# The output projection of an attention layer as seven half-size products instead of a plain product in eight quarters of the weights

## The chip, the cores and the metric

The kernel runs on one core of a Trainium2 chip. The metric is device time in microseconds (us) of one execution. TensorE does the matrix products and accumulates in PSUM; VectorE (DVE) and ScalarE (ACT) do elementwise work; GpSimd (POOL) and SyncE (SP) mostly issue DMA transfers here. Each engine works through a queue of its own in the order in which the program put the instructions there, and an instruction that waits holds everything behind it on that engine.

## The reference, cut to what matters

The model has two residual layers over 512 tokens and 1024 features. Layer 0 mixes tokens by pooling, layer 1 by attention; after each mixer comes a gated feed-forward. The change touches the last step of the attention mixer, the product of the merged heads (512 x 1024) and `w_out` (1024 x 1024):

```
merged = jnp.concatenate(
    [o_g * (N_ATTN_GROUPS * alpha[:, :, g]).astype(o_g.dtype)[:, :, None, None] for g, o_g in enumerate(outs)],
    axis=2,
).reshape(B, S, D_ATTN)
return jnp.einsum('bse,ed->bsd', merged, w_out)
...
        x = x + y
        h = rmsnorm(x, norm_ffn[i])
        x = x + swiglu(h, ffn_w_gate[i], ffn_w_up[i], ffn_w_down[i])
```

## The kernel before

All data are 32-bit floats. To keep their accuracy, each operand of a large product is split into a high part (a cast by ACT, `whi`, `bhi` or `h`) and the rest (a subtraction by DVE, `wlo`, `blo` or again `h`), and a product takes three matmuls: high by high, high by rest, rest by high. Weights pass through a queue of items of 128 x 1024 numbers (512 KB): SP loads an item into one of five buffers `wraw`, and `weights()` splits some items ahead of their use. A buffer is loaded again when its rest has been taken.

The feed-forwards already save products by a Strassen scheme (seven half-size products for eight). For it some items are sums of weight blocks, made by a DMA that adds into its destination, issued by POOL (`accum_op=ALU.add`; tiles `wraw` or `vraw`, line 138, and line 180 where one buffer is added to again after each split).

The end of the attention layer goes as follows. POOL writes the softmax weights of all heads to DRAM (`far`) and reads them back, spread over rows, into the tiles `LB0` to `LB2` and `even_rows` (line 1250). `merged(t)` for t = 0 to 7 takes the products of probabilities and values of two heads on TensorE (lines 1332 and 1334; eight products through four PSUM banks `mm`). DVE multiplies each by the weights (lines 1338 and 1342), and the result, 128 features x 512 tokens, is split into `m_hi` and `m_lo`, which are the memory of `h` (lines 387 and 388). Then `out_projection` runs: for the first 512 output columns it goes through four items of weights, each against four blocks of 128 tokens, and for the last 512 columns through four blocks of tokens, each against four items that stay split (`bhi`, `blo`). That makes 192 matmuls of 128x512 (lines 425 to 427). DVE adds each finished bank to the residual `x` (line 413), and the norm of the feed-forward follows block by block: squares (line 324), multiplication by the gain (line 333), inverse root mean square (lines 339 to 343), scaling (line 352), and transposes on TensorE (lines 366 and 358). The first feed-forward product (line 729) is next.

TensorE's order is the order in which the program is written. On the other engines a scheduler lays out the queue from its own costs and from priorities (`high_priority`).

## Time and profile before

| What | Value |
|---|---|
| median of 3 runs | 981.42 us (980.79 to 981.96) |
| the profiled execution: its time, its span | 980.24 us, 978.5 us |
| TensorE, DVE, ACT, POOL busy | 99%, 80%, 59%, 13% of the span |
| mean granted TensorE clock | 0.999 |
| DMA traffic | 163.00 MB, mean 167 GB/s |

The span is the time from the first to the last instruction of the core, and the 1.74 us between it and the execution's time lie around it. Times inside a run are counted from the span's start. A row of the timeline gives start, duration, engine, line, operation, output and inputs, a count (x2 where rows are merged), and in brackets how long the engine was idle before and what ended that. A row of the chain of waits gives start, length, engine, tile and line. The line numbers of the rows are those of the kernel before.

### The profile page before, as it was taken

Reading aid. Unit: us, or ns where it says so; the run is one execution under the profiler, and the core shown is the slowest. Engines: PE = TensorE matmul, PEld = TensorE weight load, DVE = VectorE, ACT = ScalarE, POOL = GpSimd, SP = SyncE. Lnnn points to the kernel's source line nnn. Section 1 sums busy time; section 2 is a strip of 40 time slices with the busy share of each in tenths; the row PEclk is TensorE's granted clock in tenths of the full one; section 3 lists DMA queues with packets and bytes.
Section 4 is the critical chain, followed back from the end, with each engine's and each line's share of the span. In section 5 each row is a group of like instructions: output and inputs, shape, how many; then the busy total and the mean of one; then the engine's idle time right before and its main releaser. Section 6 shows DMA issues by size and latency. Waiting matters only on the chain.

```text
span 978.5 us, 15597 instructions
## 1 busy us (share of the span) xinstructions
PE 970.9 (99%) x6028; PEld 862.6 (88%) x6028; DVE 783.9 (80%) x1083; ACT 575.3 (59%) x903; POOL 124.7 (13%) x124
## 2 busy tenths in 40 slices
PE   9999999999999999999999999999999999999997
PEld 8888899988988999889888899899998998899886
DVE  6475799888888888797897547579988898888876
ACT  6573566655665666574553554366664675567655
POOL 0002010010011111101212124101011101110110
PEclk9999999999999999999999999999999999999999
DMA  9448267479668877555221249627657947987652
GB/s 346 176 157 207 45 187 186 124 200 248 165 151 222 218 201 159 117 193 165 86 79 55 62 137 295 115 59 204 174 145 205 251 111 173 250 213 193 153 134 101
DMA packets 79466, 163.00 MB, mean 167 GB/s; under 512 B 6096, under 2 KB 6480, under 8 KB 79392
## 3 DMA queue, kind: packets, MB, share of 16 engines
q1 hardware_dynamic: 58544, 122.04, 37.6%
q0 software_dynamic: 20560, 39.69, 23.7%
q8 instruction: 47, 0.77, 0.3%
q14 instruction: 27, 0.22, 0.1%
q10 hardware_dynamic: 288, 0.27, 0.1%
HBM read 159.85 MB, written 2.13 MB: 166 GB/s over the span
## 4 chain that ended last, share of the span: by engine, by line
PE 99%; ACT 0%; DVE 0%; issue 0%; ACTq 0%
PE pair L703 32%; PE pair L847 21%; PE p L729 5%; PE mm L264 5%; PE mm L266 4%; PE mm L265 4%; PE pair L729 4%; PE r L729 2%; PE early L515 2%; PE mm L425 2%; PE mm L427 2%; PE mm L426 2%; PE mm L729 1%; PE mm L1297 1%; PE mm L1298 1%; PE mm L1299 1%
## 5 line engine op out<-in xcount | busy, mean ns | idle before, releaser
L175 DVE TENSOR_TENSOR wlo<-wraw,whi 128x1024 fp32r<-128x1024 f32 (+2 forms) x190 | 221.7, 1172 | 65.6 <-ACT whi L171 65.0
L171 ACT CAST whi<-wraw 128x1024 fp32r<-128x1024 f32 (+2 forms) x189 | 184.0, 979 | 138.4 <-PE pair L703 27.8
L171 ACT CAST whi<-vraw 128x1024 fp32r<-128x1024 f32 (+1 forms) x108 | 105.2, 980 | 117.6 <-DVE vraw L177 39.8
L175 DVE TENSOR_TENSOR wlo<-vraw,whi 128x1024 fp32r<-128x1024 f32 (+1 forms) x108 | 121.5, 1133 | 46.2 <-ACT whi L171 46.2
L703 PE MATMUL pair<-h,whi 128*128 128x512 f32 (+1 forms) x640 | 143.2, 349 | 0.0
L703 PEld LDWEIGHTS pair<-h,whi 128*128 128x128 f32 x640 | 109.1, 188 | 13.4
L703 PE MATMUL pair<-t,whi 128*128 128x512 f32 (+1 forms) x512 | 110.6, 337 | 0.0
L847 PE MATMUL pair<-whi,u_hi 128*128 128x512 f32 (+1 forms) x284 | 109.9, 387 | 0.0
L847 PE MATMUL pair<-wlo,u_hi 128*128 128x512 f32 (+1 forms) x284 | 109.9, 387 | 0.0
L847 PE MATMUL pair<-whi,u_lo 128*128 128x512 f32 (+1 forms) x284 | 109.7, 386 | 0.0
L703 PEld LDWEIGHTS pair<-t,whi 128*128 128x128 f32 x512 | 86.1, 190 | 8.4
L703 PE MATMUL pair<-h,wlo 128*128 128x256 f32 x512 | 89.2, 281 | 0.0
L703 PEld LDWEIGHTS pair<-h,wlo 128*128 128x128 f32 x512 | 76.1, 188 | 4.2
L138 POOL DMA_DIRECT2D wraw<-w x22 | 26.6, 1211 | 396.0 <-DMA wraw<-w 123.2
L177 DVE TENSOR_TENSOR vraw<-vraw,wraw 128x1024 f32<-128x1024 f32 (+1 forms) x66 | 75.2, 1139 | 0.7
L703 PE MATMUL pair<-t,wlo 128*128 128x256 f32 x384 | 71.9, 282 | 0.0
L264 PE MATMUL mm<-h,whi 128*128 128x512 f32 (+1 forms) x176 | 64.3, 365 | 0.0
L266 PE MATMUL mm<-h,wlo 128*128 128x512 f32 (+1 forms) x176 | 63.4, 360 | 0.0
L265 PE MATMUL mm<-h,whi 128*128 128x512 f32 (+1 forms) x176 | 63.4, 360 | 0.0
L847 PEld LDWEIGHTS pair<-whi,u_lo 128*128 128x128 f32 x284 | 53.3, 188 | 10.9
L847 PEld LDWEIGHTS pair<-whi,u_hi 128*128 128x128 f32 x284 | 53.4, 188 | 10.4
L847 PEld LDWEIGHTS pair<-wlo,u_hi 128*128 128x128 f32 x284 | 53.4, 188 | 10.2
(363 smaller groups left out, 2021.4 us busy)
## 6 DMA issues: line engine op xcount, KB each, us to landing
wraw<-w SPq DMA_DIRECT2D x116, 512.0 KB, 4.7
wraw<-w_down SPq DMA_DIRECT2D x32, 512.0 KB, 4.2
vraw<-w SPq DMA_DIRECT2D x22, 512.0 KB, 4.8
wraw<-w POOLq DMA_DIRECT2D x22, 512.0 KB, 6.9
vraw<-w POOLq DMA_DIRECT2D x22, 512.0 KB, 9.1
wraw<-wT SPq DMA_DIRECT2D x16, 512.0 KB, 4.4
vraw<-w_down POOLq DMA_DIRECT2D x12, 512.0 KB, 6.5
wraw<-w_down SPq DMA_DIRECT2D x24, 256.0 KB, 3.3
```

The source lines that it names most:

```text
L138: nc.gpsimd.dma_start(dst, more, accum_op=ALU.add)
L171: nc.scalar.copy(hi[:, :n], raw[:, :n])
L175: nc.vector.tensor_sub(lo[:, :n], raw[:, :n], hi[:, :n].bitcast(F32))
L177: nc.vector.tensor_add(raws[into][:, :n], raws[into][:, :n], raws[more][:, :n])
L264: nc.tensor.matmul(ps, lhsT=whi, rhs=xhi, start=first, stop=False, **kw)
L265: nc.tensor.matmul(ps, lhsT=whi, rhs=xlo, start=False, stop=False, **kw)
L266: nc.tensor.matmul(ps, lhsT=wlo, rhs=xhi, start=False, stop=last, **kw)
L425: nc.tensor.matmul(ps, lhsT=xhi, rhs=w[0][:, k, :], start=first, stop=False)
L426: nc.tensor.matmul(ps, lhsT=xhi, rhs=w[1][:, k, :], start=False, stop=False)
L703: mat = lambda o, w, m, **kw: nc.tensor.matmul(o, lhsT=w, rhs=m, skip_group_check=True, **kw)
L729: nc.tensor.matmul(ps[:, g, :], lhsT=w[:, g, c, :], rhs=right[:, z, c, :], start=i in (0, 1, 3) and g + c + k == 0, stop=c == 3 and k == 2 ...
L847: nc.tensor.matmul(acc(t), lhsT=u, rhs=w, start=first, stop=n == len(places) - 1, skip_group_check=True)
```

## The change

The projection becomes seven products of half the tokens (256), half the features (512) and half the columns (512). Write a1 and a2 for the first and second half of the tokens in the first 512 features, b1 and b2 in the last 512, and W(m,k) for the block of the weights at column half m and feature half k. The left operands are a2, a2-a1, a1-a2-b1, b1, b1-a1, b2 and a2-a1+b1-b2, formed by DVE (class `Left`). The right operands are W(0,0), W(1,0)+W(1,1), that plus W(0,0), that plus W(0,1), W(0,0)+W(1,0), W(0,1) and W(1,1). They run in the order `SEVEN` = 0, 1, 2, 5, 4, 3, 6, each as two items of weights (z = 0 in `whi`/`wlo`, z = 1 in `bhi`/`blo`). Products 1, 2 and 5 share two buffers `sraw`: after product 1's item is split, a DMA adds W(0,0) to the same buffer for product 2, and after that one's split W(0,1) for product 5. Products 0, 2, 4 and 6 accumulate in one pair of banks (`p`, in the rows `sc`), 1 and 5 in another (`r`, `mm`), 3 alone in a third (`q`, `tp`), and after each product DVE adds or subtracts both its banks to or from `x` (`flush`). The flag `SEVEN_OUT = (False, True)` selects this for the attention layer alone; layer 0 keeps its code path.

```
+SEVEN = (0, 1, 2, 5, 4, 3, 6)
+SEVEN_OUT = (False, True)
...
+            for z in range(2):
+                block = lambda m, k: by[:, order[2 * k + z] : order[2 * k + z] + 2, COLS[m]]
+                src = {0: [(0, 0)], 1: [(1, 0), (1, 1)], 3: [(0, 1)], 4: [(0, 0), (1, 0)], 6: [(1, 1)]}.get(i)
+                item = dict(kind="w" if src else "sum", shape=(2, S), rows=True, ahead=8, **({"pool": "b"} if z else {}))
...
+                if i in (1, 2):
+                    item["loads"] = (js[1][z] if i == 2 else len(queue), block(0, i - 1))
...
+        def second(self):
+            t = self.raw[0]
+            with tc.high_priority(URGENT):
+                nc.vector.tensor_sub(self.spare, t[:, :, SECOND], t[:, :, FIRST])
+                self.split(1, self.spare)
...
+                if i is None:
+                    self.next_sum(FIRST)
+                    self.split(2, self.spare)
+                    self.split(5, more[:, :, FIRST])
+                    nc.vector.tensor_sub(t[:, :, FIRST], more[:, :, FIRST], t[:, :, FIRST])
+                elif i == 0:
+                    self.split(6, t[:, :, FIRST])
+                elif i == 1:
+                    self.split(3, more[:, :, SECOND])
+                    self.next_sum(SECOND)
...
+        product(1)
+        product(2)
+        product(5)
+        for b in range(2):
+            norm.square(b, 0)
+            norm.gained(b, 0)
+        left.reserve()
+        product(4)
+        for b in range(2):
+            norm.square(b, 1)
+            norm.gained(b, 1)
+            norm.prepare(b)
+        product(3)
+        for t in range(2):
+            norm.square(2 + t, 0, q[t])
+        rests = turned_rows(norm, shift, list(enumerate(tps())))
+        ws = operands(6)
+        rests()
...
-            o = scaled_by[t % 4]
+            o = raw[t // 4][:, t % 4, :] if seven else scaled_by[t % 4]
...
+                    if t in (1, 3):
+                        left.first(t - 1)
+                    elif t == 4:
+                        left.second()
+                    elif t == 7:
+                        left.behind(None)
...
-        third = out_projection(j_wo, range(NC), m_hi, m_lo, norm, SHIFT, four, turned_banks)
+            third = seven_projection(j_wo, left, norm, SHIFT, p, r, q, lambda: (more, r), lambda: None, False)
```

Up to the end of the attention's value products the queues of all engines are as before, but for DMA issues on SP and POOL. What changes on DVE and POOL is shown at three places. In the rows, `LB` and `even_rows` are the spread weights of the heads, `pT` after the change holds the merged heads and their sums, `h` the split left operands, `sc`, `mm` and `tp` PSUM banks of the projection, `wraw` a loaded item of the projection or of the feed-forward.

DVE before, from the first merged pair of heads on:

```order
L1338 TENSOR_TENSOR o_5837<-mm_5839,LB0_5262 128x512
L388 TENSOR_TENSOR h_74<-o_5837,h_74 128x512
L1338 TENSOR_TENSOR o_5838<-mm_5859,LB1_5263 128x512
L388 TENSOR_TENSOR h_74<-o_5838,h_74 128x512
L1338 TENSOR_TENSOR odd_rows_81<-mm_5879,LB2_5264 128x512
L1342 TENSOR_TENSOR odd_rows_81<-mm_5899,even_rows_5826 128x4x128
L388 TENSOR_TENSOR h_74<-odd_rows_81,h_74 128x512
L1342 TENSOR_TENSOR o_5837<-mm_5911,even_rows_5826 128x4x128
```

DVE after, from the same place to the last merged pair:

```order
L1538 TENSOR_TENSOR pT_4231<-mm_5828,LB0_5262 128x512
L1538 TENSOR_TENSOR pT_4231<-mm_5846,LB1_5263 128x512
L183 TENSOR_TENSOR wlo_5968<-sraw_5957,whi_5967 128x1024
L423 TENSOR_TENSOR h_74<-pT_4231,h_74 128x512
L1538 TENSOR_TENSOR pT_4231<-mm_5866,LB2_5264 128x512
L1542 TENSOR_TENSOR pT_4231<-mm_5884,even_rows_5817 128x4x128
L1542 TENSOR_TENSOR pT_4231<-mm_5896,even_rows_5817 128x4x128
L522 TENSOR_TENSOR pT_4231<-pT_4231 128x1024
L423 TENSOR_TENSOR h_74<-pT_4231,h_74 128x512
L1542 TENSOR_TENSOR pT_4231<-mm_5909,LB0_5262 128x4x128
L423 TENSOR_TENSOR h_74<-pT_4231,h_74 128x1024
L1542 TENSOR_TENSOR pT_4231<-mm_5919,LB1_5263 128x4x128
```

The rest of product 1's first item (`wlo<-sraw`) now stands between the second and the third pair; the third pair's bank is read behind it. After the last row come the last pair (`LB2`), the rest of product 1's second item (`blo<-sraw`), the third sum of the left operands (line 526), its rest, the fifth sum (line 538) and the rest of b1.

DVE after, where the first products end (behind the rows just named):

```order
L578 TENSOR_TENSOR x_72<-sc_5949,x_72 128x512
L578 TENSOR_TENSOR x_72<-sc_5950,x_72 128x512
L423 TENSOR_TENSOR h_74<-pT_4231,h_74 128x1024
L580 TENSOR_TENSOR x_72<-x_72,mm_5953 128x512
L580 TENSOR_TENSOR x_72<-x_72,mm_5954 128x512
L423 TENSOR_TENSOR h_74<-pT_4231,h_74 128x1024
L526 SCALAR_TENSOR_TENSOR pT_4231<-pT_4231 128x1024
L183 TENSOR_TENSOR wlo_5978<-sraw_5957,whi_5977 128x1024
L183 TENSOR_TENSOR blo_5983<-sraw_5960,bhi_5982 128x1024
L183 TENSOR_TENSOR wlo_5991<-sraw_5957,whi_5990 128x1024
L183 TENSOR_TENSOR wlo_6032<-wraw_5987,whi_6031 128x1024
L578 TENSOR_TENSOR x_72<-sc_5949,x_72 128x512
```

DVE before, at the corresponding place:

```order
L388 TENSOR_TENSOR h_74<-o_5838,h_74 128x512
L388 TENSOR_TENSOR h_74<-odd_rows_81,h_74 128x512 x2
L175 TENSOR_TENSOR wlo_6112<-wraw_6099,whi_6111 128x1024
L175 TENSOR_TENSOR wlo_6116<-wraw_6101,whi_6115 128x1024
L175 TENSOR_TENSOR wlo_6120<-wraw_6107,whi_6119 128x1024
L175 TENSOR_TENSOR wlo_6124<-wraw_6109,whi_6123 128x1024
L413 TENSOR_TENSOR x_72<-sc_5963,x_72 128x512
```

The rests of product 2's two items (`wlo_5978`, `blo_5983`) and of product 5's first (`wlo_5991`) stand behind the flushes of products 0 and 1; before, only rests of feed-forward weights stood here. After the last row shown come the other flush of product 2 and the rest of product 5's second item.

POOL after, from the write of the heads' weights (the rows `sraw` with L144 add W(1,1), those with L188 add for products 2 and 5):

```order
L1432 DMA far_5266<-ropea_5722 64x128
L1438 DMA LB0_5262<-far_5266 64x512 x2
L1438 DMA LB1_5263<-far_5266 64x512 x2
L1438 DMA LB2_5264<-far_5266 64x512 x2
L1438 DMA even_rows_5817<-far_5266 64x512 x4
L144 DMA sraw_5957<-wT 128x2x512
L144 DMA sraw_5960<-wT 128x2x512
L1438 DMA LB0_5262<-far_5266 64x512 x2
L1438 DMA LB1_5263<-far_5266 64x512 x2
L188 DMA sraw_5957<-wT 128x2x512
L1438 DMA LB2_5264<-far_5266 64x512 x2
L188 DMA sraw_5960<-wT 128x2x512
```

POOL before, there:

```order
L1244 DMA far_5266<-ropea_5722 64x128
L1250 DMA LB0_5262<-far_5266 64x512 x2
L1250 DMA LB1_5263<-far_5266 64x512 x2
L1250 DMA LB2_5264<-far_5266 64x512 x2
L1250 DMA even_rows_5826<-far_5266 64x512 x4
L1250 DMA LB0_5262<-far_5266 64x512 x2
L1250 DMA LB1_5263<-far_5266 64x512 x2
L1250 DMA LB2_5264<-far_5266 64x512 x2
```

Now the two first adds into `sraw` stand behind the four loads of `even_rows`, and an add that waits for a rest on DVE stands ahead of the last two loads of heads' weights (`LB2`). Ahead of `far`, two adds for product 4's items (`wraw`) are new, and behind the rows shown two more adds into `sraw` follow, for product 5.

More of the change, by code (lines that the diff above doesn't have):

```diff
@@ L154, in weights @@
         for n in range(loaded["w"], min(len(queue), i + load_ahead)):
+            if queue[n].get("sums") and "s" not in pools:
+                break
             if queue[n]["kind"] == "w":
@@ L462, in out_projection, with __init__, split, first @@
         return tps
+    class Left:
+        def __init__(self, raw, spare, places):
+            self.raw, self.spare, self.places = raw, spare, places
+        def split(self, u, src, ks=(slice(0, 4),)):
+            hi, lo = self.places[u]
+            for k in ks:
+                split(hi[:, k, :], lo[:, k, :], src[:, k, :])
+        def first(self, k):
+            self.split(0, self.raw[0][:, :, SECOND], (slice(k, k + 2),))
+        def second(self):
[3 more added lines that the diff above has]
+                self.split(1, self.spare)
+        def next_sum(self, part):
+            nc.vector.scalar_tensor_tensor(
+                self.spare, self.spare, -1.0, self.raw[1][:, :, part], op0=ALU.mult, op1=ALU.subtract
+            )
+        def behind(self, i):
+            t, more = self.raw
+            with tc.high_priority(URGENT):
+                if i is None:
[8 more added lines that the diff above has]
+                    self.next_sum(SECOND)
+                elif i == 4:
+                    self.split(4, self.spare)
+        def reserve(self):
+            if 4 not in self.places:
+                self.places[4] = [
+                    wspl.tile([P, 1024], F32R, name=name).rearrange("p (k s) -> p k s", k=4) for name in ("whi", "wlo")
+                ]
@@ new lines, in seven_projection, with operands, products, flush @@
+    def seven_projection(js, left, norm, shift, p, r, q, tps, after_first, keep):
+        accs = {0: p, 1: r, 2: p, 3: q, 4: p, 5: r, 6: p}
+        def operands(i):
+            return [weights(j, split_ahead=6, held=z + (i in (4, 3, 6))) for z, j in enumerate(js[i])]
+        def products(i, ws, ts=range(2)):
+            hi, lo = left.places[(0, 1, 2, 3, 6, 5, 4)[i]]
+            places = [(z, t, c) for z in range(2) for t in ts for c in range(2)]
+            for z, t, c in places:
+                whi, wlo = (w[:, c, :] for w in ws[z])
+                uhi, ulo = (u[:, 2 * z + c, t * P : (t + 1) * P] for u in (hi, lo))
+                for k, (u, w) in enumerate(((uhi, whi), (uhi, wlo), (ulo, whi))):
+                    first, last = (i < 2 or i == 3 and not keep) and (z, c, k) == (0, 0, 0), (z, c, k) == (1, 1, 2)
+                    nc.tensor.matmul(accs[i][t], lhsT=u, rhs=w, start=first, stop=last, skip_group_check=True)
+        def flush(i, t):
+            half, n, sign = {0: (0, 2, 1), 1: (1, 0, -1), 2: (0, 0, 1), 3: (0, 2, 1), 4: (1, 0, -1), 5: (0, 0, 1), 6: (1, 2, -1)}[i]
+            at = x[:, n + t, COLS[half]]
+            with tc.high_priority(URGENT):
+                if sign > 0:
+                    nc.vector.tensor_add(at, accs[i][t], at)
+                else:
+                    nc.vector.tensor_sub(at, at, accs[i][t])
+        def product(i):
+            products(i, operands(i))
+            for t in range(2):
+                if i:
+                    flush(i, t)
+            left.behind(i)
+        products(0, operands(0))
+        after_first()
+        left.behind(0)
+        with tc.high_priority(URGENT):
+            for t in range(2):
+                if keep:
+                    nc.scalar.copy(q[t], p[t])
+                else:
+                    flush(0, t)
+        product(1)
[11 more added lines that the diff above has]
+        product(3)
+        for t in range(2):
+            norm.square(2 + t, 0, q[t])
+        rests = turned_rows(norm, shift, list(enumerate(tps())))
+        ws = operands(6)
+        rests()
+        for t in range(2):
+            norm.gained(2 + t, 0)
+            products(6, ws, (t,))
+            flush(6, t)
+            norm.square(2 + t, 1, p[t])
+            norm.gained(2 + t, 1)
+            if t == 0:
+                norm.prepare(2)
@@ L1346, in trunk_kernel @@
         for t in range(8):
-            cast, rest = merged(t)
-        for j in (j_wo[-1] + 1, j_wo[-1] + 2):
-            queue[j].update(cast_behind=cast.ins, behind=rest.ins)
+            done = merged(t)
+        if not seven:
+            for j in (j_wo[-1] + 1, j_wo[-1] + 2):
+                queue[j].update(cast_behind=done[0].ins, behind=done[1].ins)
         norm = Norm(2, mp.tile([P, D], F32, name="even_rows"))
```

114 lines of the change are left out of this document (92 added, 22 removed).

## The prediction

> **What bounds the kernel now.** I read the page's first part and its chain first, then what TensorE waited for.
>
> ```profile
> span 978.5 us, 15597 instructions
> PE 970.9 (99%) x6028; PEld 862.6 (88%) x6028; DVE 783.9 (80%) x1083; ACT 575.3 (59%) x903; POOL 124.7 (13%) x124
> PE 99%; ACT 0%; DVE 0%; issue 0%; ACTq 0%
> PE mm L302 <- DVE odd_rows L296: 1.1, 1, 1.1
> ```
>
> TensorE is the bound everywhere: its only wait in the whole span is 1.1 us, at the start (last row). So fewer matmuls shorten the run by their whole time, as long as everything that feeds them stays ahead. The next views are therefore the chain around the projection, and the busy time of each engine there (columns: PE, PEld, DVE, ACT, POOL).
>
> ```profile
> 602.30 0.43 PE sc L425
> 640.60 0.65 PE sc L366 x16
> 641.25 0.50 PE tp L366 x16
> 647.41 0.88 PE mm L358 x8
> 648.29 2.84 PE p L729 x24
> 602.30:648.30 46.00, 46.00 (x234) 38.06 (x235) 28.04 (x51) 19.90 (x35) 6.14 (x5) 1.00 0.58 134
> 650.00:690.00 40.00, 40.00 (x338) 40.00 (x337) 39.34 (x55) 28.28 (x41) 3.63 (x3) 1.00 0.65 184
> ```
>
> The projection occupies 602.30 to 648.29, with DVE busy for 28.04 of 46.00 us; right behind it, in the feed-forward, DVE is full (39.34 of 40). The spare 18 us are all that new DVE work can use before that.
>
> **The gain.** 8 x 24 = 192 matmuls become 7 x 24 = 168. Two starts, 120 matmuls apart, give the price of one: 27.20 / 120 = 0.2267 us.
>
> ```profile
> 609.16 0.39 PE L425 MATMUL sc<-whi,h 128*128 128x512 f32 x1
> ...
> 636.36 0.39 PE L425 MATMUL mm<-bhi,h 128*128 128x512 f32 x1
> ```
>
> 24 x 0.2267 = **5.44 us** less. The transposes are as many as before; the eight for the third token block only come after the first feed-forward product.
>
> **The new work on DVE and ACT.** Prices, by the step from one start to the next:
>
> ```profile
> 595.11 0.68 DVE L1338 TENSOR_TENSOR o<-mm,LB 128x512 f32<-128x512 f32 x1
> 597.09 0.69 DVE L1338 TENSOR_TENSOR o<-mm,LB 128x512 f32<-128x512 f32 x1
> 599.67 1.13 DVE L1342 TENSOR_TENSOR odd_rows<-mm,even_rows 128x512 f32<-128x512 f32 x1
> 600.62 0.70 DVE L388 TENSOR_TENSOR h<-odd_rows,h 128x512 fp32r<-128x512 f32 x1
> 611.09 2.35 DVE L175 TENSOR_TENSOR wlo<-wraw,whi 128x1024 fp32r<-128x1024 f32 x2
> 621.15 1.28 DVE L413 TENSOR_TENSOR x<-sc,x 128x512 f32<-128x512 f32 x2
> 609.41 1.99 ACT L171 CAST whi<-wraw 128x1024 fp32r<-128x1024 f32 x2
> 633.56 1.15 ACT L352 ACTIVATE even_rows<-even_rows,r 128x1024 f32<-128x1024 f32 x1 [0.74 <-DVE r L343]
> ```
>
> A 128x1024 pass costs DVE 1.13 (2.35 less the first's 1.22), a 128x512 one 0.60, a merged pair with rows put in another order 0.90 to 0.95, a cast on ACT 0.95. The change adds six rests of weights (6.8), replaces eight half-size rests of the merged heads by seven full ones (7.9 - 4.8 = 3.1), adds four sums (4.5) and six flushes (3.6): 18.0 us on DVE. With the 28.04 there, that is 46.0 us in a stage which would last 46.0 - 5.44 = 40.6. Some of it lies ahead of the stage, but the order of the queue decides more than the sum. ACT's 8 us more find room (19.90 of 46 busy), so I cost them only where a cast stands in a chain.
>
> **The new waits on DMA.** The two first items of product 1 need an add by DMA, which POOL issues only behind the heads' weights; products 2 and 5 need two more adds in series with the splits.
>
> ```profile
> 584.00 0.55 POOL L1244 DMA_DIRECT2D far<-ropea  x1 [5.95 <-ACT ropea L1243]
> 587.23 3.13 POOL L1250 DMA_DIRECT2D LB<-far  x6 [2.68 <-DMA far<-ropea]
> 592.42 1.16 POOL L1250 DMA_DIRECT2D even_rows<-far  x2 [1.04 <-DMA LB<-far]
> 607.78 1.07 DVE L1342 TENSOR_TENSOR odd_rows<-mm,LB 128x512 f32<-128x512 f32 x1 [0.68 <-DMA LB<-far]
> L180 POOL DMA_DIRECT2D vraw<-w_down x6: 1188/1298/1506, 402.0 to 937.1; - x6
> DMA to landing us min/median/max: 5.6/7.1/7.8
> ...
> L138 POOL DMA_DIRECT2D wraw<-w x22: 1188/1203/1316, 77.6 to 889.2; - x22
> DMA to landing us min/median/max: 4.0/7.3/13.4
> ...
> L1250 POOL DMA_DIRECT2D LB<-far x12: 516/526/571, 587.2 to 600.6; - x12
> DMA to landing us min/median/max: 4.9/7.1/8.1
> ```
>
> The nearest row for such an add is L180, the same add after a split: 7.1 us from issue to landing, which I take; the ends are 4.0 (the fastest of L138) and 9.1, the page's median for `vraw<-w` from POOL:
>
> ```profile
> vraw<-w POOLq DMA_DIRECT2D x22, 512.0 KB, 9.1
> ```
>
> Here the Trainium skill speaks for a cheaper change: DMA: Bandwidth & Descriptors, section Anatomy of one DMA — SWDGE (gpsimd) path, puts a transfer at about 2.0 us plus its bytes over 436 GB/s, an estimated 3.2 us for 512 KB, and the sum by it would be about +7 us for the +14.6 below. The trace does not agree for adds: none landed under 4.0.
>
> **The walk through the queues**, starting from the times of before, since all queues are the same up to there:
>
> 1. POOL is free at 593.6; first add at 594.0, landed 601.1, cast 602.1, its rest on DVE done at 603.2. That rest stands behind the second merged pair (597.09 + 0.60 = 597.7), so DVE idles until 602.1, and behind it wait a half split and the third and fourth pair: banks free at 604.4 and 605.3, with which TensorE finishes the merge (two pairs at 0.9) at 606.2. Loss: 606.2 - 602.3 = **3.9 us**.
> 2. DVE goes on without rest to 610.9 (up to the seventh pair: 2 x 0.60, 0.95 + 0.90, 1.13, 0.60, 0.90, 1.13, 0.90). The add for product 2 stands on POOL ahead of the last `LB2` loads and waits for the rest of 603.2, so the last load goes out at 604.9 and lands at 612.0; last pair done 612.9. Then, before product 2's first rest is done: nine passes (10.2), four flushes (2.4), one wait for a cast (0.95): 626.4. TensorE has finished products 0 and 1 (10.9) at 617.1, and can do one matmul of product 2. Loss: 626.4 - 617.1 - 0.2 = **9.1 us**.
> 3. The add for product 5 may start only now: landed 633.5, cast 634.5, rest 635.6. Product 2 has ended at 631.6. Behind it a rest, two flushes of product 2 and the rest of product 5's second item: 639.1, where product 5 waits again; it ends at 641.6. Loss: 641.6 - 631.6 - 5.4 = **4.6 us**.
> 4. Products 4 and 3 run through, to 652.5. The scaling of blocks 0 and 1 stands on ACT behind a square of product 3's result: flush 0.6, square with its read 0.8, first scaling 1.15, second 1.05, half the transposes 0.5: product 6 starts at 656.6, against 652.5 + 1.15. Loss: **2.9 us**.
>
> Sum: 3.9 + 9.1 + 4.6 + 2.9 - 5.4 = +15.1. By the clock of the walk product 6 ends at 656.6 + 5.4 = 662.0, where the projection of before ended at 647.41: **+14.6 us**, which I take (the stage of before holds 0.4 us of starts beyond its 43.5 of matmuls and 1.15 of transposes, which the sum counts as kept). The feed-forward's loads by SP wait for buffers that free late (product 4's first rest at 636.7), but its first rest needs to be ready only at 662, so nothing. Its full DVE starts with up to 2.9 us more queued (two passes and a flush); TensorE never waited there, so I take 0 and keep 2.9 for the range. Against the profiled execution's own 980.24 that gives 994.8; the median of the runs shown is 1.2 higher, so **996 us**.
>
> The clock is a second rule to weigh: the rows say 1.00 wherever I looked, with no gap of TensorE beyond 1.1 us. TensorE: Matmul & The Clock Gate, section Part 1, says that after an idle window of some 3.4 us the clock is halved until some 3.4 us of work have passed, about 1.7 us lost per gap, as an estimate from the page. By it the sum rises by 0 to 3.4 us, as the loss behind the gaps of steps 1 and 2 is hidden in the next wait. No run here shows it.
>
> **Rivals.**
>
> *Everything stays covered*: 981.4 - 5.4 = 976.0, faster. For it: TensorE's single wait and 18 us of idle DVE. It decides at DVE's row of product 2's first rest: it must be done by 613.2 (602.3 + 10.9). Even with adds that land at once, DVE goes from 597.7 to 607.4 for the last pair and to 620.9 for that rest: 7.7 lost there and 2.9 at the transposes, 5.2 more than before, 986.6. So it needs DVE's passes to be shorter than in any row here. 8 in 100.
>
> *Waits that just eat the gain*, within 2 us of before (979.4 to 983.4): the same mechanism with half its losses. 4 in 100.
>
> *Adds at the fastest row*, 4.0 us, loads of heads' weights at 4.9: step 1 shrinks by 3.1, step 2 starts 4.2 earlier in all, step 3 shrinks by 3.1 more: +7.3, 988.7; with step 4 covered 986. 17 in 100.
>
> *The queues lock further*: adds at 9.1 (2.0 in each of the two series), the last `LB2` load another 1 us late, 2.9 us in the feed-forward: 1004 and more. 8 in 100.
>
> **How the numbers follow.** The forecast (990 to 1003) has 63 in 100. The range 985 to 1004 takes in the fast adds and leaves out the covered case, most of the balanced one and what lies beyond the locked queues, not over 2 in 10. About 0.2% (2 us) is what a measurement of this kernel can tell from no change: slower 0.88, same 0.04, faster 0.08.
>
> **What would show it.** Right: TensorE waits of about 4, 9, 4 and 3 us at the last merged pairs, product 2, product 5 and the transposes; the first two put down to DVE, product 5's to the rest behind the add into `sraw`; the first DVE row of `sraw` near 602; adds into `sraw` near 7 us; feed-forward rows from 662 on at the old pace, the first `p` product about 14 us late. Wrong: a first rest of `sraw` before 598, no wait of TensorE at product 2, or passes over `pT` well under 1.13 us. The change did not do what it says if TensorE's matmuls in the projection aren't 168.

## The result, and the profile after

The changed kernel takes 1009.15 us (median of 5 runs, 1005.84 to 1010.38) against 980.79 us before (5 runs, 980.37 to 981.96): ratio 1.0282, 95% interval 1.026 to 1.0303. The profiled execution took 1007.74 us with a span of 1006.0, 27.5 us more than the span before; 14.6 were forecast, and the time lies outside the range given. The page of the changed kernel, its span, busy times and granted clock in 40 slices:

```profile
span 1006.0 us, 15591 instructions
...
PE 975.3 (97%) x6004; PEld 863.5 (86%) x6004; DVE 800.7 (80%) x1099; ACT 583.6 (58%) x909; POOL 134.8 (13%) x132
...
PEclk9999999999999999999999997889999999999999
```

TensorE has 24 instructions fewer (6028 before, 6004 now), as announced, and is busy 4.4 us longer: a part of its work ran at a lower clock (three slices show 7 or 8). What TensorE waited for, in the changed kernel:

```profile
PE mm L1532 <- DVE pT L1538: 8.4, 1, 8.4
PE sc L571 <- DVE wlo L183: 5.5, 1, 5.5
PE mm L393 <- ACT even_rows L387: 2.6, 1, 2.6
PE pair L914 <- ACT keep L966: 2.0, 1, 2.0
PE mm L401 <- ACT even_rows L387: 1.9, 1, 1.9
...
```

In the order of time these are the seventh merged pair (L1532), product 2 (L571), the transposes of blocks 0 and 1 (L401), those of block 2 in the feed-forward (L393), and a product of the feed-forward (L914). The rows of TensorE where the waits end, with the first matmul of the merge (594.14), of the projection (613.53) and of the feed-forward (668.40); the last row is the first matmul of the feed-forward in the kernel before:

```profile
594.14 0.66 PE L1532 MATMUL mm<-pT,v 128*64 128x128 f32 x8
...
609.92 3.68 PE L1532 MATMUL mm<-pT,v 128*64 128x128 f32 x32 [8.35 <-DVE pT L1538]
613.53 0.80 PE L571 MATMUL sc<-whi,h 128*128 128x512 f32 x1
...
631.39 0.79 PE L571 MATMUL sc<-wlo,h 128*128 128x512 f32 x1 [5.48 <-DVE wlo L183]
...
643.66 0.50 PE L571 MATMUL mm<-blo,h 128*128 128x512 f32 x1 [0.48 <-DVE blo L183]
...
668.40 0.50 PE L914 MATMUL p<-h,whi 128*128 128x256 f32 x2 [0.41 <-ACT sc L359]
...
648.04 0.48 PE L729 MATMUL p<-h,whi 128*128 128x256 f32 x2
```

Three stretches follow: the merge (594.14 to 613.53) takes 19.4 us and took 9.1 (593.12 to 602.23), the projection up to the feed-forward's first product 54.9 for 45.8, and what comes after it 337.6 for 330.5 (0.8 of that are the eight transposes of block 2, which moved there). That is 26.5 of the 27.5 us; the other 1.0 lies ahead of the merge, which begins that much later. How the merge came to its 19.4 us stands on POOL, in the rows of its DMA issues in the changed kernel:

```profile
578.68 1.26 POOL L144 DMA_DIRECT2D wraw<-wT  x1
583.25 1.22 POOL L144 DMA_DIRECT2D wraw<-wT  x1 [3.31 <-DVE den L1421]
584.17 0.88 POOL L1432 DMA_DIRECT2D far<-ropea  x1
593.01 3.14 POOL L1438 DMA_DIRECT2D LB<-far  x6 [7.96 <-DMA far<-ropea]
...
598.32 2.54 POOL L144 DMA_DIRECT2D sraw<-wT  x2
```

Product 4's two adds (`wraw<-wT`) were issued at 578.68 and 583.25, ahead of the write of the heads' weights `far`. That write is 32 KB; its first reader went out at 593.01, 8.8 us behind its issue, where the kernel before needed 3.2 (584.00 to 587.23). So the first add into `sraw` went out at 598.32 instead of the forecast's 594.0. The casts and rests of the weights in `sraw`, on ACT and DVE of the changed kernel:

```profile
606.36 1.04 ACT L179 CAST whi<-sraw 128x1024 fp32r<-128x1024 f32 x1 [11.94 <-DMA sraw<-wT]
...
607.44 1.23 DVE L183 TENSOR_TENSOR wlo<-sraw,whi 128x1024 fp32r<-128x1024 f32 x1 [8.46 <-ACT whi L179]
...
630.12 1.22 DVE L183 TENSOR_TENSOR wlo<-sraw,whi 128x1024 fp32r<-128x1024 f32 x1
...
638.91 1.22 DVE L183 TENSOR_TENSOR wlo<-sraw,whi 128x1024 fp32r<-128x1024 f32 x1 [6.44 <-ACT whi L179]
```

ACT stood 11.94 us at the cast, DVE 8.46 at its rest, and the merged pairs behind them stood too. Product 2's first rest came at 630.12, product 5's at 638.91. For product 2 it was not the add that was late: its weight was cast by 616.1, but DVE, which from 607.44 on stood idle for only 1.2 us in all, reached the rest 14 us later, behind the merged pairs, sums and flushes queued ahead of it.

### The profile page after: what moved, and what is told of

Its sections match the earlier page's. It is cut to its first block, busy times and chain, and to the rows that moved or that the text cites. A ratio compares the mean times of both kernels' runs of the same rounds, so it can differ in the third digit from the quotient of the medians.

```text
span 1006.0 us, 15591 instructions
## 1 busy us (share of the span) xinstructions
PE 975.3 (97%) x6004; PEld 863.5 (86%) x6004; DVE 800.7 (80%) x1099; ACT 583.6 (58%) x909; POOL 134.8 (13%) x132
## 5 line engine op out<-in xcount | busy, mean ns | idle before, releaser
L144 POOL DMA_DIRECT2D wraw<-w x22 | 26.6, 1209 | 388.0 <-DMA wraw<-w 112.7
L1032 PEld LDWEIGHTS pair<-whi,u_lo 128*128 128x128 f32 x284 | 53.3, 188 | 10.7
```

The source lines that it names most:

```text
L144: nc.gpsimd.dma_start(dst, more, accum_op=ALU.add)
L1032: nc.tensor.matmul(acc(t), lhsT=u, rhs=w, start=first, stop=n == len(places) - 1, skip_group_check=True)
```

## The experiments

Median times, ratios to the kernel before with their intervals, and from each profile the three stretches: from the first matmul of the merge to the first of the projection, from there to the first product `p` of the feed-forward, and the remainder of the span. Two kernels' medians differ by chance by up to some 2.5 us (the intervals are 0.2 to 0.4% wide), so smaller effects are read from the stretches.

| Kernel | median us | ratio (95% interval) | merge | projection | remainder |
|---|---|---|---|---|---|
| before | 980.79 | 1 | 9.1 | 45.8 | 330.5 |
| changed | 1009.15 | 1.0282 (1.026 to 1.0303) | 19.4 | 54.9 | 337.6 |
| 1 no adds | 978.03 | 0.9976 (0.9966 to 0.9987) | 9.1 | 41.6 | 332.4 |
| 2 no first adds | 997.34 | 1.0161 (1.0138 to 1.0184) | 15.7 | 47.7 | 335.3 |
| 3 no adds in series | 995.86 | 1.0146 (1.0129 to 1.0164) | 19.8 | 47.7 | 332.5 |
| 4 `far` first | 1004.47 | 1.0255 (1.0239 to 1.0271) | 15.2 | 56.1 | 337.8 |
| 5 rests behind the merge | 1009.23 | 1.0294 (1.0276 to 1.0312) | 19.7 | 57.6 | 337.6 |
| 6 casts and rests behind | 1005.14 | 1.0256 (1.0241 to 1.0272) | 11.3 | 59.1 | 338.5 |
| 7 three orders | 1003.27 | 1.0224 (1.0206 to 1.0242) | 12.9 | 57.0 | 337.7 |
| 8 four orders | 998.12 | 1.0173 (1.0155 to 1.0191) | 9.1 | 56.3 | 335.0 |
| 9 late cast behind | 1006.68 | 1.0262 (1.0242 to 1.0282) | 19.1 | 55.2 | 337.7 |
| 10 transposes late | 1001.74 | 1.022 (1.0206 to 1.0234) | 19.4 | 53.1 | 334.3 |
| 11 busy in the merge's gap | 1006.18 | 1.0266 (1.025 to 1.0282) | 19.0 | 53.3 | 338.6 |
| 12 busy ahead of product 2 | 1008.79 | 1.0292 (1.0277 to 1.0308) | 18.9 | 55.2 | 337.6 |
| 13 sums in DRAM, 22 DMAs | 1016.67 | 1.0355 (1.0333 to 1.0376) | 18.1 | 42.6 | 339.1 |
| 14 sums in DRAM, 12 DMAs | 991.03 | 1.011 (1.0093 to 1.0127) | 17.5 | 42.4 | 333.0 |
| 15 the same, rests behind | 997.17 | 1.0167 (1.0153 to 1.0181) | 17.7 | 46.2 | 338.0 |
| 16 the same, casts too | 987.54 | 1.0079 (1.0066 to 1.0093) | 9.1 | 48.2 | 335.2 |

The theory was the forecast's: late adds and the queues behind them. The first three runs take adds away.

**1, without any of the eight adds.**

```
-    src = {0: [(0, 0)], 1: [(1, 0), (1, 1)], 3: [(0, 1)], 4: [(0, 0), (1, 0)], 6: [(1, 1)]}.get(i)
+    src = {0: [(0, 0)], 1: [(1, 0)], 3: [(0, 1)], 4: [(0, 0)], 6: [(1, 1)]}.get(i)
...
-    if i in (1, 2):
+    if False:
```

> The changed kernel without its eight adds by DMA: the sums of the projection's weights are replaced by their first block, so the output is not the reference's; every matmul, pass of DVE and cast stays. Theory A (the waits of products 1, 2 and 5 hang on the landing of the adds, and far's delay on the adds ahead of it): the waits of 8.4 us at the merge and at product 5 go, far lands in 3 us, only DVE's longer chain is left (5 to 8 us at product 2) and what follows the projection: 988 to 995 us. Rival B (DVE's added passes alone make the loss): the wait at the merge moves to product 2, 1001 to 1006 us. If everything were covered without the adds: 976.

It took 978.03 us, 31 less than the changed kernel and 0.24% less than before. TensorE's three longest waits in it (a fourth is 0.3), and the projection's row by stretches (PE, PEld, DVE, ACT, POOL busy):

```profile
PE mm L393 <- ACT even_rows L387: 1.1, 1, 1.1
PE mm L337 <- DVE odd_rows L331: 1.1, 1, 1.1
PE mm L401 <- ACT even_rows L387: 1.0, 1, 1.0
...
601.40:643.00 41.60, 40.20 (x203) 32.65 (x202) 40.64 (x60) 26.20 (x39) 4.88 (x4) 1.00 0.50 136
```

DVE is full in the projection (40.64 of 41.60 us), and TensorE hardly waits. So rival B falls. Theory A is right about the cause and too small: it left 5 to 8 us at product 2 for DVE, and the time is nearer to the 976 of the third case. With the adds gone nearly all the added passes, casts and flushes are covered, and the eight adds with what they do to the queues are the whole loss. The scheduler laid DVE's and ACT's queues out differently here (four rests of `sraw` stand ahead of the merge, which late adds don't allow), so 31 us is the price of the adds together with that.

**2 and 3, without the first adds, and without those in series.** Run 2 has only the change of `src` for i = 1, run 3 only the `if False`.

> The changed kernel without the two adds of product 1's weights, which are the first block alone (so its output is not the reference's); the four adds in series and product 4's two stay. Theory (each group of adds has its own share, the first one blocks DVE's queue at the merge): the first rest of sraw is done before 595, the wait at the seventh merged pair falls from 8.4 to 2 to 4 us (what is left is far's late landing), product 2 still waits 4 to 9 us for the adds in series: 997 to 1003. Rival (the series alone sets the end, the first adds are hidden by it): within 2 us of 1009.

> The changed kernel without the four adds that follow in series in product 1's tiles (products 2 and 5 take product 1's weights, so its output is not the reference's); product 1's own two adds and product 4's two stay. Theory: the wait of 8.4 us at the merge stays, those at product 2 (5.5) and product 5 (1.3) go or fall under 2 us, SP and DVE are ahead again in the feed-forward: 993 to 1000. Rival (DVE's passes behind the late merge make product 2's wait, adds or not): product 2 still waits 4 us or more, 1002 to 1006.

997.34 and 995.86 us, 11.8 and 13.3 less than the changed kernel. In run 2 the wait at the merge fell to 3.9, TensorE stood 2.7 us at the merge's start, and of the projection's waits one of 1.6 us at product 5 was left. The 4 to 9 us that the theory kept for product 2 did not come: its first rest, now the late one, stood on DVE ahead of merged pairs (606.84, behind 4.8 us idle), and its price was paid at the merge. In run 3 the waits at the merge and at product 2 were 8.8 and 5.0. So both groups cost much, and in run 3 rival and theory are each half right: product 2's wait stays without an add of its own, as the rival said, so it is DVE's queue behind the late merge (DVE is busy for 21.27 of the 21.30 us from 608.50 to 629.80, where product 2's first rest starts); the waits at product 5 are gone, and the remainder behind the projection is as short as without any adds (332.5), as the theory said.

**4, the write of `far` first.** Product 4's adds are issued behind the last load of the heads' weights; on DVE, ACT and SP next to nothing moves.

```
-            nc.gpsimd.dma_start(dst, more, accum_op=ALU.add)
+            with tc.issue_after(last_of_far[0]) if item.get("late_add") else nullcontext():
+                nc.gpsimd.dma_start(dst, more, accum_op=ALU.add)
...
+                if i == 4:
+                    item["late_add"] = True
```

> The changed kernel, with product 4's two adds issued by POOL behind the last load of the heads' weights instead of ahead of the far write. Theory (the small far write landed in 8.8 us instead of 2.9 because two 512 KB adds were ahead of it on POOL's queue): far lands within about 3.5 us of its issue, the first sums add is issued near 594 instead of 598.3, TensorE's wait at the seventh merged pair shrinks from 8.4 us to 3 to 5, and the run takes 1001 to 1004 us against the 1009 of the changed kernel. Rival (the chain of DVE passes and the sums adds set the end of the merge and of product 2's wait anyway): far lands sooner, but waits of 8 and 5 us become 4 and 9, and the run stays at 1007 to 1010.

POOL's rows and the wait at the merge in this kernel:

```profile
583.46 0.55 POOL L1436 DMA_DIRECT2D far<-ropea  x1 [5.33 <-ACT ropea L1435]
...
587.09 3.12 POOL L1442 DMA_DIRECT2D LB<-far  x6 [3.08 <-DMA far<-ropea]
...
593.48 2.52 POOL L146 DMA_DIRECT2D sraw<-wT  x2 [0.76 <-PE mm L1491]
...
PE mm L1536 <- DVE pT L1542: 4.5, 1, 4.5
```

`far` was read 3.6 us behind its issue instead of 8.8, the first add went out at 593.48, and the merge is 4.2 us shorter: the 32 KB had waited for the adds ahead of it. The median is 4.7 us lower, 0.5 above the range of the theory, and the two intervals still touch. The rival has a part in it: the projection grew by 1.2 us, with waits of 6.4 and 1.3 at product 2 for the 5.5 of the changed kernel. A page bears on this: the Trainium skill's DMA: Bandwidth & Descriptors, section Queues, rings and completion order, says that a DMA engine takes turns, a packet at a time, between the queue rows that have work for it. These rows agree with it, since the adds and the write were all POOL's, and no turn between rows could bring the write forward.

**5 and 6, what stands in the queues at the merge.** Run 5 holds product 1's rests behind the eighth merged pair on DVE; run 6 also holds their casts on ACT behind the cast of the first difference of merged heads.

```
+            for i, z in {7: [(1, 0), (1, 1)]}.get(t, ()):
+                queue[j_wo[i][z]]["behind"] = scaled.ins
...
+                for i, z in [(1, 0), (1, 1)]:
+                    queue[j_wo[i][z]]["cast_behind"] = self.cast
```

> The changed kernel with one order on DVE changed: the rests of product 1's two weights stand behind the eighth merged pair instead of behind the second; all DMAs, casts and passes stay. Theory A (the wait of 8.4 us at the merge is DVE's queue standing for 8.5 us behind a rest whose add had not landed, with the pairs behind it ready): that wait falls under 3 us, DVE's later passes and the first rest of product 2 (630.1) come 5 to 8 us earlier, and the run takes 1001 to 1004 us. Theory B (the adds in series set the end of the projection whatever DVE does first): what is won at the merge is waited for at products 1, 2 and 5, and the run stays within 2 us of 1009.

> As the kernel with product 1's rests behind the eighth merged pair on DVE, and now the casts of the same two weights stand on ACT behind the cast of the first difference of merged heads. In the kernel with the rests alone the wait of 8.5 us stayed, and its rows put it to ACT: the cast of sraw, 12.8 us at the head of ACT's queue, stood ahead of the merged heads' cast for which DVE's next rest waited. Theory A (two queues have to be cleared, not one): the wait at the merge falls under 3.5 us, product 2's first rest comes 3 us earlier or more, and the run takes 1000 to 1005 us. Theory B (the adds in series set the end whatever stands ahead): the waits move to products 1, 2 and 5, and the run stays at 1006 to 1010.

Run 5: 1009.23 us, the wait still 8.5. Theory A as written fell. The rows of that kernel on ACT and DVE:

```profile
606.35 1.04 ACT L179 CAST whi<-sraw 128x1024 fp32r<-128x1024 f32 x1 [12.84 <-DMA sraw<-wT]
...
607.94 0.69 DVE L423 TENSOR_TENSOR h<-pT,h 128x512 fp32r<-128x512 f32 x1 [8.33 <-ACT h L422]
```

DVE's next instruction is now a rest of merged heads, and it waits for ACT, which still stands at the cast of the late weight. Run 6 clears both queues: the wait at the merge is 1.8 us, the merge 11.3 instead of 19.4. Yet the run is only 4.0 us shorter, between the ranges of the two theories, since the projection grew to 59.1, with waits of 2.4 and 6.1 us at the two halves of product 1. So theory A holds for the place of the wait (two queues, not one), theory B for most of its price.

**7 and 8, orders together.** Run 7 has the orders of runs 4, 5 and 9, run 8 those of 4, 6 and 9. Nothing is computed otherwise.

> Three changes of order together: product 4's two adds behind the last load of the heads' weights on POOL, product 1's rests behind the eighth merged pair on DVE, and the first late cast of the feed-forward behind block 2's scaling on ACT; nothing is computed otherwise. If their gains add up (about 5, 6 and 2.5 us of different waits): 994 to 998. If the adds in series become the bound: 1000 to 1004. Since these four adds stay, not under 990 in either case.

> Only orders changed, four together: product 4's adds behind the last load of the heads' weights on POOL, product 1's casts and rests behind those of the merge on ACT and DVE, the first late cast of the feed-forward behind block 2's scaling. If the gains add up: 991 to 997. If the four adds in series, 6 to 8 us each from issue to landing, are the bound then: 998 to 1003, with waits of 4 us or more at products 2 and 5 and none over 1.5 at the merge.

1003.27 and 998.12 us. Run 8's merge is that of the kernel before (9.1 us), and its projection 56.3. Its first add on POOL, and TensorE's waits at product 1 (two rows) and product 5 (two rows):

```profile
591.96 2.52 POOL L146 DMA_DIRECT2D sraw<-wT  x2 [0.50 <-DMA LB<-far]
...
608.44 0.50 PE L577 MATMUL mm<-wlo,h 128*128 128x512 f32 x1 [1.09 <-DVE wlo L185]
617.57 0.79 PE L577 MATMUL mm<-blo,h 128*128 128x512 f32 x1 [6.12 <-DVE blo L185]
633.09 0.49 PE L577 MATMUL mm<-bhi,h 128*128 128x512 f32 x1 [1.43 <-ACT bhi L181]
634.35 0.50 PE L577 MATMUL mm<-blo,h 128*128 128x512 f32 x1 [0.77 <-DVE blo L185]
```

From the issue of the first add to the last rest of product 5 it takes 634.35 - 591.96 = 42.4 us; in the changed kernel 643.66 - 598.32 = 45.3, in run 4 46.6, in run 6 41.8. This series (three adds in one tile, each with a cast and a rest behind it) took 42 to 47 us in all of them. Not all of it is DMA: in run 8 product 1's second weight was cast by 604.4, but DVE came to its rest only at 616.30, 9 us behind the first (607.18), with other passes between, so some 12 us of the series are the order of DVE's queue. No run moves that rest forward, and how short the series could get is open. Behind it come 23.4 us of work (634.35 to `p` at 657.71). With the first add at 592 and the series at this length the projection ends at 657.7, where it ended at 648.0 before. That is what runs 6 to 8 ran into: the gains did not add up, and runs 7 and 8 came out in the ranges of their second expectations. The places of run 8's waits were expected wrongly: 7.2 us stand at product 1, and only 0.6 and 2.2 at products 2 and 5.

**9 and 10, the feed-forward and the transposes.** Run 9 holds the cast of the first late weight (`vraw`) of the feed-forward behind the scaling of block 2 on ACT. Run 10 places the transposes of blocks 0 and 1 behind the first half of product 6; the rows that they read are by then partly overwritten with block 2's, so its time is that of an order, not of the same computation.

```
+                queue[j_ffn[1][0][0][1]]["cast_behind"] = norm.scaled.ins
```

> The changed kernel, with one order on ACT changed: the cast of the first late weight of the feed-forward (its vraw lands by 669.4) stands behind the scaling of block 2 instead of ahead of it. Theory (TensorE's wait of 2.6 us at the transposes of block 2, and the half clock behind it, come from that cast standing in ACT's queue for its add): that wait falls under 0.5 us and the run is 2.5 to 4.5 us shorter, 1004.5 to 1006.5. Rival (the feed-forward's DVE is full, so the time comes back at the next late operand): the wait of 2.0 us at the pair product near 720 grows by as much, and the run stays within 1 us of 1009.

> The changed kernel, with the transposes of blocks 0 and 1 behind the first half of product 6 instead of ahead of the whole of it. Theory (the 1.9 us of wait there are ACT's scaling behind the square of product 3's result, and the clock was granted at 0.66 behind it): half a product, 2.7 us, covers it, and the run is 2 to 3 us shorter, 1006 to 1007. Rival (the blocks' later transposes only push the feed-forward's first operands, and the scaling of block 2 stands later): within 0.8 us of 1009.

Run 9 has a median 2.5 us lower, but its remainder is 337.7 us, as in the changed kernel. Its waits at the two places of the feed-forward:

```profile
PE pair L915 <- ACT keep L967: 2.9, 1, 2.9
PE mm L393 <- ACT even_rows L387: 0.4, 1, 0.4
```

The first of the expected waits went (2.6 to 0.4), the other grew (2.0 to 2.9): so the rival, as far as the stretch shows it, and a median that the intervals don't tell from no change. Run 10 is 7.4 us shorter, more than either said, 3.3 of it in the remainder; as its transposes no longer wait for the same data, it shows no more than that waits at the transposes reach the feed-forward. One more kernel has the sums in DRAM (as in run 13) and the transposes behind that half product, with block 2's gain behind them:

> As the kernel with sums made beforehand in DRAM, and the first half of product 6 stands on TensorE ahead of the transposes of blocks 0 and 1, with the gain of block 2 behind them. Theory (what is left there is ACT's scaling behind the square of product 3's result, 1 to 2 us, and half a product of 2.7 us covers it): 1 to 2 us less than that kernel, 975 to 978. Rival (block 2's gain, square and scaling come later by as much, and its transposes in the feed-forward wait instead): no gain, or up to 2 us more than that kernel.

1016.67 us, the same as run 13: no gain, as its rival said. Which late cast costs the feed-forward its 5 to 6 us is not settled.

**11 and 12, the clock.** Both put matmuls of the unit matrix into a gap.

```
+            if seven and t == 6:
+                keep_warm(four[0], 16)
```

> The changed kernel with 16 more matmuls on TensorE (the unit matrix by itself, into a bank that the projection overwrites) ahead of the seventh merged pair, in the gap of 8.4 us; on DVE three instructions of the projection change places. Both theories: the 64 matmuls of the last two pairs take about 1.8 us instead of 3.6, and the projection starts at the full clock. Theory A (the half clock behind the gap is on the path): the run is 2 to 3 us shorter, 1006 to 1007. Theory B (what is won there is waited for at product 2, whose first rest DVE gives at the same time): the wait of 5.5 us at product 2 grows by as much, and the run stays within 1 us of 1009.

> The changed kernel with 11 such matmuls ahead of product 2, in its gap of 5.5 us; the other engines' order stays the same up to product 2's rests. Both theories: product 2's 24 matmuls take 5.4 to 5.8 us instead of 7.5. Theory A (that half clock is on the path): the run is about 2 us shorter, 1007. Theory B (product 5 starts when its add has landed and its rest is done, 638.9, whatever TensorE did): the wait ahead of product 5 grows from 0.8 to about 2.8 us and the run stays within 0.8 us of 1009.

In run 11 the matmuls filled only half of the gap, 4.2 us were left, and the 32 matmuls behind it took 3.68 us as before: what both theories expected did not happen, so it tells nothing. In run 12 they left 3.24 us of the 5.5. TensorE's rows around product 2 there:

```profile
631.90 0.50 PE L571 MATMUL sc<-wlo,h 128*128 128x512 f32 x1 [3.24 <-DVE wlo L183]
...
639.47 0.49 PE L571 MATMUL mm<-whi,h 128*128 128x512 f32 x1 [0.41 <-ACT whi L179]
```

The half clock came later and for less long: product 2's matmuls from 631.90 on took 7.0 us (to 638.9) instead of 7.5, and product 5 started at 639.47, 0.5 later than in the changed kernel (638.93). The run stayed at 1008.79. What little was won there was waited for, as theory B said.

**13 to 16, the sums made beforehand.** The sums are built in DRAM where POOL has no work, and SP loads them. Run 13 builds all four sums from their blocks (22 DMAs of 512 KB from 403 us on). Runs 14 to 16 chain three of them (12 DMAs, six at 100 us and six at 404), have three tiles for sums instead of two, and product 4's adds late. Run 15 holds late rests on DVE, run 16 also casts on ACT.

```
+                        nc.gpsimd.dma_start(dst, whole[:, at : at + 2, COLS[m]], **(dict(accum_op=ALU.add) if n else {}))
...
+                item.update(kind="w", src=[summed[i, z]], sums=True)
```

> The changed kernel with the same four sums of weights (two half items each) made beforehand: 22 DMAs on POOL build them in DRAM from 403 us on, where POOL has no work for 38 us, and the projection loads them by SP like any other weight; no add by DMA is left between 575 and 650. Theory (the loss is the landing of the adds and their places on POOL's queue; the passes on DVE are covered): no wait of TensorE over 1.5 us at the merge and at product 2, and the run takes 976.5 to 980 us. Rival A (the two tiles for sums force the loads into a series, each behind a rest of DVE, 5 to 8 us each): TensorE waits 2 to 5 us at product 5, 981 to 986. Rival B (22 more DMAs slow the loads of the stage where they run): waits near 405 to 445, 982 or more.

> The sums of products 1, 2 and 5 made beforehand in DRAM again, in 12 DMAs instead of 22 and in two gaps of POOL (6 behind the add of 99.6 us, 6 behind those of 402), each sum copied from the one before it; three tiles for sums in the projection instead of two; product 4's two adds behind the last load of the heads' weights. Theory (22 DMAs filled POOL's queue: 8 went out at once and the rest one every 4.6 us, which held back POOL's rope adds by 22 us; 6 in a gap fit its queue): no wait near 445 to 480, waits under 1.5 us at the merge and product 2, 976.5 to 980. Rival A (even 6 hold the feed-forward's adds back): waits near 140 or 445, 982 to 990. Rival B (the loads of the second and third sum still come in series behind DVE): waits of 2 to 5 us at products 2 and 5, 981 to 986.

> The kernel with the sums chained in DRAM (12 DMAs, three tiles), and two orders on DVE: the second rest of product 2 behind the sixth merged pair, those of product 5 behind the eighth. Theory (its 5.3 us of waits at the merge are again DVE standing 5.5 us at a rest whose load landed late, at 600.7): the wait at the merge falls under 1.5 us and the run takes 979 to 985 us against the 991 of that kernel. Rival (the rests come too late for products 2 and 5): waits of 2 to 5 us there, 986 to 991.

> The kernel with the sums chained in DRAM (12 DMAs, three tiles), and the late ones' casts (second of product 2, both of product 5, both of product 4) held on ACT behind casts of merged heads, their rests on DVE behind the sixth and eighth merged pairs, and the feed-forward's late cast behind block 2's scaling. With the rests alone it went to 997 from 991. Theory (a late load's cast at the head of ACT's queue, and its rest on DVE, are all that is left): no wait over 1.5 us at the merge, 978 to 984 us. Rival (casts that wait for a free tile now stand ahead of merged heads' casts, and products 2 or 5 wait for those): 985 to 990.

Run 13 is the slowest of all, 1016.67 us, in the range of its rival B, though the wait came later than that said (it ends at 484.26); its loads in series were late too, but stalled the merge (5.2 us) and not product 5, as rival A had it. POOL's issues of the sums there, and TensorE's longest wait:

```profile
404.10 2.38 POOL L1198 DMA_DIRECT2D sum<-wT  x2
407.50 1.33 POOL L1198 DMA_DIRECT2D sum<-wT  x2 [1.02 <-issue]
410.19 2.01 POOL L1198 DMA_DIRECT2D sum<-wT  x3 [1.36 <-issue]
412.81 0.65 POOL L1198 DMA_DIRECT2D sum<-wT  x1 [0.61 <-issue]
415.89 1.08 POOL L1198 DMA_DIRECT2D sum<-wT  x1 [2.43 <-issue]
...
467.74 1.04 POOL L1198 DMA_DIRECT2D sum<-wT  x1 [2.17 <-issue]
...
477.64 1.73 POOL L1224 TENSOR_TENSOR ropeb<-ropeb,angles 128x512 f32<-128x512 f32 x1
...
PE sc L1257 <- DVE k L1230: 12.9, 1, 12.9
```

Eight went out within 9 us, then POOL itself stood at each issue, one per 4.7 us (415.89 to 467.74, eleven steps), and its adds for the attention's rotation began at 477.64 instead of 454.87 in the changed kernel. With 12 DMAs in two gaps (run 14) that is gone, TensorE has no wait there, and the run takes 991.03 us; left are 5.3 us at the merge, again ACT and DVE at the cast and rest of a sum that landed late (600.7). No expectation of run 14 had a time above 990. Holding back the rests alone made it worse (run 15, 997.17, above both of its ranges: a wait of 6.7 us at the merge, ACT still standing at the cast); in run 5 it had not helped either. With the casts held too (run 16) the merge takes the 9.1 us of before, and the run 987.54. Its longest waits:

```profile
PE mm L407 <- ACT even_rows L393: 3.6, 1, 3.6
PE pair L925 <- ACT keep L977: 2.9, 1, 2.9
```

So the theory (late loads at the head of two queues) holds for the merge, but not for the time, which falls into the rival's range; product 2 or 5 hardly waits, though, and what is left lies at the transposes and in the feed-forward; 987.54 is still 0.8% above the kernel before. Only the kernel that leaves the adds out was faster than before, by 0.24%; no version that computes the same sums was.

## Why the prediction was right in its direction and too small

**The gain.** Right within 0.7 us: run 1's projection is 4.2 us shorter than before, of which 0.8 are the moved transposes, and 1.3 of new waits at the other transposes stand against it, which makes 4.7 for the 5.44 of 24 matmuls.

**The series of steps 1 to 3.** The forecast walked from the first add at 594.0 to the last rest of product 5 at 639.1, 45.1 us. Measured: 598.32 to 643.66, 45.3. The mechanism, its places and its length were right, DVE's long queue ahead of product 2's rest included. The single waits were 8.4, 5.5 and 1.2 us, with 2.9 and 2.3 of half clock behind the first two, for losses of 3.9, 9.1 and 4.6: the late start was paid at the merge already.

**Step 1 failed in its start.** "POOL is free at 593.6" took the queues up to there as those of before. Product 4's two adds stand on POOL right ahead of the write of `far`; they are named ahead of the prediction, but the rows of POOL's queue shown there begin one row behind them, and no term of the sum priced them. They made `far` land 5.6 us later and the first add 4.3. Run 4 shows it.

**The clock failed as a term costed at nothing.** The forecast let the halved clock vanish in the next wait, 0 to 3.4 us. At product 2 that is right by run 12, if weakly. Behind the last rest of product 5 no wait is left to hide in: from there to `p` it took 24.7 us (643.66 to 668.40) against the forecast's 22.9. Of these 1.8 us, 1.1 are product 6 at a lower clock (661.27 to 667.83, 6.56 us for 5.44) and 0.6 the gap ahead of `p`, a wait for ACT that the forecast did not have. The row ahead of the transposes, then a stretch of 3 us behind them, and two of 5 us at the ends of the two long gaps; the granted clock, third number from the end, was 0.59 and 0.50:

```profile
659.18 0.71 PE L401 MATMUL mm<-ident,even_rows 64*128 64x64 f32 x16 [1.86 <-ACT even_rows L387]
...
661.00:664.00 3.00, 3.00 (x16) 2.37 (x13) 3.00 (x7) 1.71 (x4) 2.19 (x2) 0.59 1.06 247
...
610.00:615.00 5.00, 5.00 (x36) 4.38 (x37) 5.00 (x6) 1.87 (x3) 1.44 (x3) 0.50 0.86 159
...
630.00:635.00 5.00, 3.61 (x9) 2.83 (x10) 2.48 (x3) 0.00 (x0) 2.42 (x2) 0.50 0.24 22
```

**The feed-forward failed as a term taken at 0.** Its remainder grew by 7.1 us, 6.3 without the moved transposes: waits of 2.6 and 2.0, and lower clock behind them. The forecast had looked whether the first rest is ready in time; what came late were later weights. SP loaded the first three items `vraw` of the feed-forward at 656.61, 11.8 us ahead of the first `p`, where the kernel before had 45.7 (602.34), and POOL issued the last of their adds as late as this:

```profile
668.17 1.20 POOL L144 DMA_DIRECT2D vraw<-w  x1 [3.92 <-DMA vraw<-w]
```

That is 0.2 us ahead of `p`; in run 3, without the adds in series, it is 9.8 us ahead (652.50), and 5.1 of the 7.1 us are gone. So the adds in series cost the feed-forward most of its loss. That they do it through these late loads is what the rows suggest; no run moves the loads alone.

These terms make the miss: the late start and the series 4.3 + 0.2, the work behind the series 1.8, the feed-forward 6.3, together 12.6, where 27.5 - 14.6 = 12.9 are missing.

**Step 4** was right in its sum: 1.86 and 0.33 us of wait at the transposes and 0.8 us by which the transposes themselves took longer, for 2.9.

**The rivals.** That everything stays covered was put at needing shorter passes of DVE, with 986.6 at best for adds that land at once. Run 1 says 978.0: with the weights of products 1, 2 and 5 in place early (and not summed) the passes do fit, because DVE has free time ahead of the projection (18.48 of 26.40 us busy from 575.00 to 601.40 in run 1), which the forecast's fixed queue did not use. "The queues lock further", 1004 and more, is what came, but not by its adds of 9.1 us: the four in series landed in 5.8 to 7.9, median 6.6, a little under the 7.1 taken. Its 2.9 us in the feed-forward were of the right kind and too few. The estimate of 3.2 us per 512 KB from the Trainium skill (DMA: Bandwidth & Descriptors, Anatomy of one DMA — SWDGE (gpsimd) path) does not hold for these adds, which ran beside other transfers: the fastest took 5.8.

## What to carry to other kernels

Before a DMA is added to a queue, read what stands behind it in that queue, however small: 32 KB behind two adds of 512 KB landed 5.6 us later, and the first add that waited for them started 4.3 us later than forecast. A late operand blocks every engine at whose head one of its instructions stands, so both the cast's and the rest's queue have to be cleared, and then the next chain (here a series of adds in one buffer and the passes between them, 42 to 47 us long) is the bound; first price the change without that chain altogether. Where TensorE was full before, a new gap can also cost half the clock for some time behind it (2.9 and 2.3 us were lost behind the two longest here, 1.1 in product 6), and the stage that follows needs its own walk through all queues.

## What the runs showed of the hardware

- In run 13 POOL took eight DMAs from DRAM to DRAM of 512 KB within 9 us and then one per 4.7 us for twelve more. It stood at the issue itself ("issue" in the brackets: nothing that the profile shows was waited for). With six in a gap (run 14) its adds for the rotation began at 454.84, as in the changed kernel.
- The clock behind a gap of TensorE is not told by the gap's length alone. Behind 8.4 and 5.5 us it was 0.50 (shown above). Behind 1.48 us ahead of the transposes it was 0.50 in run 5 (663.3 to 665.5) and 1.00 in run 7 (657.3 to 660.3). Behind 1.86 us and 32 small transposes it fell to 0.59 in the changed kernel (shown above), and in run 8 it stayed at 1.00 behind the same gap and transposes:

```profile
649.87 0.71 PE L405 MATMUL mm<-ident,even_rows 64*128 64x64 f32 x16 [1.85 <-ACT even_rows L391]
...
651.00:654.00 3.00, 3.00 (x27) 2.49 (x28) 3.00 (x7) 2.40 (x6) 1.64 (x2) 1.00 1.05 264
```

The Trainium skill's TensorE: Matmul & The Clock Gate, Part 1, says that the activity is counted in free-running windows of some 3.4 us; gaps of the same length with different outcomes agree with that. The forecast, which by that page counted only idle times of some 3.4 us, was too kind.
